# A two-layer trunk on one core: even-odd tiles written in a row, 1/rms by Newton steps, and a resting gate lane

## The chip, the core and the metric

The kernel runs on one core of a Trainium2 chip. The core has a matrix engine (TensorE, PE in the profile), a vector engine (VectorE, DVE), an activation engine (ScalarE, ACT), GpSimd (POOL) and the engine SyncE (SP), whose queue issues the weight DMAs here. Each engine works through its own queue in order and waits on semaphores of the others. SBUF is the memory that all of them share; PSUM holds the sums that TensorE writes. The metric is the device time of one execution in microseconds; lower is better.

## What is computed

272 tokens (16 learned ones in front of 256) of 2048 features go through two layers. The reference, cut to its frame:

```python
def rms_norm(x, g):
    y = x * lax.rsqrt(jnp.mean(x * x, axis=-1, keepdims=True) + EPS)
    return y * g

def mixer_ab(h, ...):                       # layer 0
    q, f, i, g, sx, sb, sc = split_cols(h @ w_in, AB_SIZES)
    o = rms_norm(hgrn2_chunked(q, f, i, lb), out_norm_g) * jax.nn.silu(g)
    yb = sb * causal_depthwise_conv(sc * sx, sconv_w)
    return jnp.concatenate([o, yb], axis=-1) @ w_out

def mixer_cd(h, ...):                       # layer 1
    rx, ry, q, ckv, iq, ik, iw = split_cols(h @ w_in, CD_SIZES)
    u = causal_depthwise_conv(rx, conv_w) + conv_b
    hc = rg_lru(u, w_a, b_a, w_i, b_i, lam) * jax.nn.gelu(ry)
    att = dsa_attention(q, rms_norm(ckv, kv_norm_g), iq, ik, iw, w_uk, w_uv)
    return jnp.concatenate([hc, att], axis=-1) @ w_out

def swiglu(h, w1, w3, w2):
    return (jax.nn.silu(h @ w1) * (h @ w3)) @ w2

for l in range(2):
    h = h + rms_norm(mixer(rms_norm(h, ln_mix_pre[l])), ln_mix_post[l])
    h = h + rms_norm(swiglu(rms_norm(h, ln_ffn_pre[l])), ln_ffn_post[l])
return h[:, 16:]
```

`rg_lru` makes two gates per block of 128 channels, `r = sigmoid(u @ w_a + b_a)` and `ig = sigmoid(u @ w_i + b_i)`, and runs a linear recurrence over time with them. `dsa_attention` selects for each token the best 64 keys by an indexer's scores, and attends to these and to the learned tokens.

## The kernel before

Everything is kept with features on the 128 partitions and tokens along the free dimension: the residual stream is 16 tiles `h[k]` of 128x272. The weights are float32. To keep precision, each weight tile (`raw`, 128x1024, that is four blocks of 128 input rows by 256 output columns) is split into a high and a low part: ScalarE casts it to the rounded format (`whi`, L128), VectorE subtracts (`wlo`, L129). Inputs are split the same way (`xh`, `xl`). Each product is then three matmuls, `whi·xh`, `whi·xl`, `wlo·xh` (L200 to L202 in `group`), so a weight tile is 24 matmuls. There are six buffers for each weight part, seven for `raw`, and eight PSUM banks.

*Even-odd layout.* A split input holds the tokens with even numbers in its first half and those with odd numbers in its second. `woven(t)` is the view that goes through such a tile in the order of tokens (one element of the first half, one of the second, and so on), and `pairs(t)` is a plain tile in the matching shape. TensorE reads the tile through `woven`. In the kernel before the engines also write it through `woven`: the source is read in a row, and consecutive results go alternately to the two halves. The places are `pre` (L305 on ScalarE, L306 on VectorE: the entering input of a stage, 16 tiles per stage), `split_ahead` (L399, L400), `split` with `weave` (L236, L237: hidden tiles of SwiGLU in layer 0, the mixers' outputs), the copies of the values `v` (L1203, L1205), and one sum at the end (L1342).

*Stages.* There are four: mixer and SwiGLU of each layer. `start_stage` brings the residual up to date and splits it, tile by tile, while the first group's matmuls run (`pre`; per tile on VectorE `upd` L439, `h` L440 and `xl` L306, on ScalarE `xh` L305), and then takes the squares for the norm (`squares`). The norm's factor is applied behind the matmuls, so TensorE needs it late: the second group of products carries four hooks, of which the third sums the squares by a matmul (`stat`, L262), forms 1/rms (`inverse_rms`), and the fourth spreads it over partitions by a matmul (`spread`, L288) and copies it (`scale`, L347). `inverse_rms` writes mean square plus epsilon on VectorE (`ms`, L275) and raises it to the power -1/2 on GpSimd (`rms`, L279). It is called for the four stages' own norms, for the norm of the latent in layer 1 (`latent_scale`), and three times with `more` given, for the norm of a stage's output.

*Order.* TensorE runs in the order in which the program is written. On the other engines a scheduler orders the instructions, with `issue_after` as a tool of the program: an instruction made under it is put behind a named one on its engine. `later(i)` makes such a list from `self.urgent` for the weight splits of a group; for groups that start no stage `i` is -1.

*Lanes.* Layer 1's small work is written as generators in three lanes. `pump(n)` takes `n` steps from the first lane that is not empty, between chunks of weights. Lane 0 is the indexer's selection (`select`: `sc`, top-8 rounds L1029, L1030, `bias` L1035), lane 1 the recurrence's gates (`rg_gates`: convolution `u` L965, L967, matmuls `rgr` L971 and `rgi` L972, sigmoids, `rd` L981) and its scan. A lane's "wait" step counts as nothing. The selection is pumped through the groups of the key weights (`wuk`, 1 step per chunk) and the value products (`vacc`, L1199 to L1201).

*End.* The last output halves are summed, normed and written by `finish(b)`, whose DMAs are at L1362. Before the last `finish`, `forms` (L1301) runs 50 matmuls into a PSUM tile that nothing reads.

Of the kernel before, what the change touches and what calls it, by code (L numbers as in the profile page):

```python
# [52 lines left out]

class Trunk:
# [3 lines left out]
    def __init__(self, ctx, tc):  # L58
# [15 lines left out]
        self.copies = []  # L74

# [152 lines left out]
    def split(self, src, n, name, weave=False):  # L228
        hi = self.slot(name + "h", F32R)
        lo = self.slot(name + "l", F32R)  # L230
        if weave:
            hi, lo, src = woven(hi[:, :n]), woven(lo[:, :n]), pairs(src)
            at = slice(None)
        else:
            at = (slice(None), slice(0, n))
        self.nc.scalar.copy(hi[at], src)  # L236
        self.nc.vector.tensor_tensor(lo[at], src, hi[at].bitcast(F32), op=ALU.subtract)  # L237
# [3 lines left out]
    def rsqrt(self, v, shape, mk):  # L241
# [8 lines left out]
        for _ in range(3):  # L250
# [3 lines left out]
            V.scalar_tensor_tensor(b, a, 1.5, y, op0=ALU.add, op1=ALU.mult)  # L254
# [15 lines left out]
    def inverse_rms(self, sums, n, nfeat, more=None):  # L270
# [21 lines left out]
    def streamed(self, j, k, lo_t):  # L292

        return (woven(x[j][:, k, :])[:, lo_t // 2 :, :] for x in (self.xhi, self.xlo))

    def pre(self, k, lo_t, layer, which, update, xs):
# [10 lines left out]
        self.made = a, v  # L307
# [12 lines left out]
        xs.append((xh, xl))  # L320
# [34 lines left out]
    def start_stage(self, m, parts1, parts2, lo_t, layer, which, n, factors, update=None, between=None):  # L355
# [11 lines left out]

        accs1 = self.group(parts1, xg, n, before=before, between=between, begun=begun)
# [23 lines left out]
    def split_ahead(self, m, layer, which, lo_t):  # L392

        nc = self.nc
        for k in range(4):
            g = self.gain(which, layer, k)
            for j, src in (2, self.h[k][:, lo_t:T]), (3, m["m"][k][:, : T - lo_t]):
                xh, xl = self.streamed(j, k, lo_t)
                nc.scalar.activation(xh, pairs(src), AF.Copy, scale=g)  # L399
                nc.vector.scalar_tensor_tensor(xl, pairs(src), g, xh.bitcast(F32), op0=ALU.mult, op1=ALU.subtract)  # L400
# [680 lines left out]
    def mixer_cd(self, a, m):  # L1081
# [96 lines left out]
        for g in range(QFIRST):  # L1178
            queries(g)
        for g in range(4):  # L1180
# [10 lines left out]
        for g in range(2):  # L1191
            raw = self.fetch([(0, 0, wuv[:, 512 * g : 512 * (g + 1)].rearrange("(k p) c -> p k c", p=P))], 2, 512)
            hi, lo = self.whole(raw, 2, 512)
            for i, (t0, n) in enumerate(TOK[T]):
# [8 lines left out]
                S.copy(woven(vs[i][32:48, c] if i == 2 else vs[i][:, c]), pairs(ps[:n, :]))  # L1203
                if i == 1:
                    S.copy(woven(vs[2][:NM, c]), pairs(ps[:NM, :]))  # L1205
                self.pump(1)
        while self.lanes[0]:
            self.pump(1)
        for g in range(QFIRST):
# [205 lines left out]
```

## Time and profile before

| | us |
|---|---|
| device time, median of 3 runs (2305.86 to 2308.21) | 2305.95 |
| the profiled execution | 2310.25 |
| its span | 2308.5 |
| TensorE busy | 2277.6 (99%) |
| VectorE busy | 1511.5 (65%) |
| ScalarE busy | 1127.6 (49%) |
| GpSimd busy | 109.7 (5%) |
| weight DMAs | 414 MB, 179 GB/s read over the span |

The profiled execution took 4.3 us more than the median. TensorE is the engine that works nearly all the time, and the weight stream has room: DMA engines are busy 59% of the span. What a change can win is TensorE's idle time, its time at the lower of its two clock levels, and nothing else unless matmuls are removed. A mean over the span says little here, because the idle time lies in a few places.

### The profile page before, as it was taken

To read this page: it belongs to the slowest core of one execution; us is meant where nothing else is said; L and a number is where in the kernel's file an instruction comes from. 1 tells how busy PE (TensorE), PEld (TensorE's weight loads), DVE (VectorE), ACT (ScalarE), POOL (GpSimd) and SP (SyncE) were. 2 spreads that over 40 slices of the span, in tenths; PEclk is the share of its full clock that TensorE was granted. 3 is DMA by queue.
4 is the path that set the end of the run, shared out by engine and by line. 5 is a ranking of instruction groups with operands and counts; after the bars stand their busy time and mean duration, and the time that the engine had idled before them with its cause. 6 is when DMAs were issued, how large, how long until landed. Compare 5 with 4: busy or idle time off the path is not lost.

```text
span 2308.5 us, 45101 instructions
## 1 busy us (share of the span) xinstructions
PE 2277.6 (99%) x18613; PEld 2217.1 (96%) x18613; DVE 1511.5 (65%) x2441; ACT 1127.6 (49%) x1628; POOL 109.7 (5%) x142
## 2 busy tenths in 40 slices
PE   9999999999999999999999998999999999999999
PEld 8999999989999999999998997999999899989998
DVE  8767677586654555566668798767665456656655
ACT  6443445564444444344456567656444444444443
POOL 1422100000000000000000000200000000000000
PEclk9999999999999999999999999999999999999999
DMA  8554556636666665666564644464666666666663
GB/s 265 155 152 138 156 173 187 200 121 194 188 191 191 189 188 179 194 199 188 176 202 120 207 137 147 146 200 136 205 199 197 204 196 199 199 202 196 198 205 106
DMA packets 402856, 416.98 MB, mean 181 GB/s; under 512 B 15551, under 2 KB 379562, under 8 KB 402650
## 3 DMA queue, kind: packets, MB, share of 16 engines
q1 hardware_dynamic: 402506, 413.95, 59.0%
q8 instruction: 146, 2.39, 0.4%
q14 instruction: 60, 0.49, 0.1%
q10 hardware_dynamic: 144, 0.15, 0.0%
HBM read 411.95 MB, written 2.10 MB: 179 GB/s over the span
## 4 chain that ended last, share of the span: by engine, by line
PE 94%; DVE 3%; ACT 1%; POOL 1%; issue 1%; DMA 0%; SPq 0%; DVEq 0%
PE acc L200 27%; PE acc L201 26%; PE acc L202 26%; PE acc L1261 3%; PE acc L1260 3%; PE acc L1259 3%; DVE xl L306 1%; ACT xh L305 1%; PE lev L702 1%; POOL rms L279 1%; DVE h L440 0%; DVE wlo L129 0%; PE idx L1011 0%; PE forms L1301 0%; PE acc L416 0%
## 5 line engine op out<-in xcount | busy, mean ns | idle before, releaser
L129 DVE TENSOR_TENSOR wlo<-raw,whi 128x1024 fp32r<-128x1024 f32 (+2 forms) x791 | 954.8, 1210 | 655.2 <-ACT whi L128 638.3
L128 ACT CAST whi<-raw 128x1024 fp32r<-128x1024 f32 (+2 forms) x791 | 815.1, 1032 | 1023.3 <-PE acc L201 769.7
L200 PE MATMUL acc<-xh,whi 128*128 128x272 f32 (+1 forms) x4248 | 1193.5, 281 | 3.7 <-DVE pt L556 1.8
L201 PE MATMUL acc<-xl,whi 128*128 128x272 f32 (+1 forms) x4248 | 1184.6, 279 | 7.2 <-DVE xl L306 7.1
L202 PE MATMUL acc<-xh,wlo 128*128 128x272 f32 (+1 forms) x4248 | 1182.2, 278 | 0.0
L201 PEld LDWEIGHTS acc<-xl,whi 128*128 128x128 f32 x4248 | 811.2, 191 | 11.9 <-DVE xl L306 11.3
L200 PEld LDWEIGHTS acc<-xh,whi 128*128 128x128 f32 x4248 | 811.2, 191 | 9.5 <-ACT xh L305 3.9
L202 PEld LDWEIGHTS acc<-xh,wlo 128*128 128x128 f32 x4248 | 811.3, 191 | 0.0
L200 PE MATMUL acc<-hidh,whi 128*128 128x272 f32 x704 | 196.7, 279 | 0.0
L201 PE MATMUL acc<-hidl,whi 128*128 128x272 f32 x704 | 196.6, 279 | 0.0
L202 PE MATMUL acc<-hidh,wlo 128*128 128x272 f32 x704 | 196.6, 279 | 0.0
L1259 PE MATMUL acc<-whi,hidh 128*128 128x512 f32 (+1 forms) x380 | 139.0, 366 | 0.0
L1261 PE MATMUL acc<-wlo,hidh 128*128 128x512 f32 (+1 forms) x380 | 138.3, 364 | 0.0
L1260 PE MATMUL acc<-whi,hidl 128*128 128x512 f32 (+1 forms) x380 | 138.3, 364 | 0.0
L200 PEld LDWEIGHTS acc<-hidh,whi 128*128 128x128 f32 x704 | 133.2, 189 | 0.0
L201 PEld LDWEIGHTS acc<-hidl,whi 128*128 128x128 f32 x704 | 133.2, 189 | 0.0
L202 PEld LDWEIGHTS acc<-hidh,wlo 128*128 128x128 f32 x704 | 133.2, 189 | 0.0
L1261 PEld LDWEIGHTS acc<-wlo,hidh 128*128 128x128 f32 x380 | 72.1, 190 | 8.6
L1259 PEld LDWEIGHTS acc<-whi,hidh 128*128 128x128 f32 x380 | 72.1, 190 | 8.4
L1260 PEld LDWEIGHTS acc<-whi,hidl 128*128 128x128 f32 x380 | 72.1, 190 | 8.3
L279 POOL TENSOR_TENSOR rms<-ms,minus_half 128x3 f32<-128x3 f32 (+1 forms) x8 | 18.1, 2268 | 1080.4 <-DVE ms L277 929.2
L305 ACT ACTIVATE xh<-h,pt 128x272 fp32r<-128x272 f32 (+1 forms) x48 | 33.5, 760 | 22.2 <-DVE h L440 21.7
(366 smaller groups left out, 2180.2 us busy)
## 6 DMA issues: line engine op xcount, KB each, us to landing
raw<-in_ffn_w_dram SPq DMA_DIRECT2D x518, 512.0 KB, 3.7
raw<-in_ab_w_in_dram SPq DMA_DIRECT2D x110, 512.0 KB, 3.6
raw<-in_cd_w_in_dram SPq DMA_DIRECT2D x68, 512.0 KB, 4.3
raw<-in_ab_w_out_dram SPq DMA_DIRECT2D x28, 512.0 KB, 3.5
raw<-in_cd_w_out_dram SPq DMA_DIRECT2D x28, 512.0 KB, 4.0
raw<-in_ffn_w_dram SPq DMA_DIRECT2D x17, 256.0 KB
raw<-in_ab_w_out_dram SPq DMA_DIRECT2D x8, 256.0 KB, 3.0
raw<-in_cd_w_out_dram SPq DMA_DIRECT2D x8, 256.0 KB, 4.5
```

The lines of the kernel that those rows point to most:

```text
L128: nc.scalar.copy(hi[at], raw[at])
L129: nc.vector.tensor_tensor(lo[at], raw[at], hi[at].bitcast(F32), op=ALU.subtract)
L200: nc.tensor.matmul(o, lhsT=hi[:, kk, c : c + m], rhs=xh, start=k == 0, stop=False)
L201: nc.tensor.matmul(o, lhsT=hi[:, kk, c : c + m], rhs=xl, start=False, stop=False)
L202: nc.tensor.matmul(o, lhsT=lo[:, kk, c : c + m], rhs=xh, start=False, stop=k == nk - 1)
L279: i = self.nc.gpsimd.tensor_tensor(r[:, :w], self.ms[:, :w], self.minus_half[:, :w], op=ALU.pow)
L305: a = nc.scalar.activation(xh, pairs(h), AF.Copy, scale=g)
L306: v = nc.vector.scalar_tensor_tensor(xl, pairs(h), g, xh.bitcast(F32), op0=ALU.mult, op1=ALU.subtract)
L702: nc.tensor.matmul(ps[:M, j * half : (j + 1) * half], lhsT=k[:, j * P : j * P + M], rhs=upper(qh[:, j * P : (j + 1) * P]), start=True, sto ...
L1259: self.nc.tensor.matmul(o, lhsT=xh, rhs=wh, start=k == 0, stop=False)
L1260: self.nc.tensor.matmul(o, lhsT=xl, rhs=wh, start=False, stop=False)
L1261: self.nc.tensor.matmul(o, lhsT=xh, rhs=wl, start=False, stop=k == nk - 1)
```

## The change

Four things are edited.

1. *Layout written in a row.* `halves(t)` is a tile as two contiguous halves, and `apart(t)` a plain tile with its even elements first. The splits now write through `halves` and read the source through `apart`, with a stride of two elements. What is stored where is the same, and TensorE reads it through `woven` as before. `pre` and `split_ahead` share a new helper `enter`.
2. *1/rms by Newton steps.* Without `more`, `inverse_rms` calls `rsqrt` (a function that the kernel has for another norm): a shift and a subtraction on the bits give a first guess, three Newton steps follow, eleven small VectorE instructions, each on the result of the one before. Its last instruction is kept in `self.hold`, and until the next stage starts `later(-1)` puts the weight splits of ordinary groups behind it (their VectorE instruction `wlo`; the cast on ScalarE has nothing to be put behind there).
3. *The gate lane rests.* During the groups of the key weights and the value products `self.awake` is 1, so `pump` serves lane 0 alone; then 3 again.
4. *`forms` is gone*, with its 50 matmuls.

```diff
+def apart(t):
+    return t.rearrange("p (j a) -> p a j", a=2)
+def halves(t):
+    return t.rearrange("p (a j) -> p a j", a=2)
...
     def pump(self, n):
-        for lane in self.lanes:
+        for lane in self.lanes[: self.awake]:
...
                 if i >= first:
                     ctx.enter_context(self.tc.issue_after(ins.ins))
+            if self.hold and i < 0:
+                ctx.enter_context(self.tc.issue_after(self.hold.ins))
             yield
...
         if weave:
-            hi, lo, src = woven(hi[:, :n]), woven(lo[:, :n]), pairs(src)
-            at = slice(None)
+            h, l, src = halves(hi[:, :n]), halves(lo[:, :n]), apart(src)
+            hi, lo = woven(hi[:, :n]), woven(lo[:, :n])
...
-        r, w = self.tiny("rms"), len(TOK[n])
+        w = len(TOK[n])
+        if more is None:
+            r = self.rsqrt(self.ms[:, :w], (P, w), lambda name, dtype: self.tiny(name, (P, 8), dtype))
+            self.hold = self.last_root
+            return r
+        r = self.tiny("rms")
         i = self.nc.gpsimd.tensor_tensor(r[:, :w], self.ms[:, :w], self.minus_half[:, :w], op=ALU.pow)
-        if more is not None:
-            self.urgent.append((6, i))
+        self.urgent.append((6, i))
...
+    def enter(self, j, k, lo_t, src, g):
+        h, l = (halves(x[j][:, k, :])[:, :, lo_t // 2 :] for x in (self.xhi, self.xlo))
+        a = self.nc.scalar.activation(h, apart(src), AF.Copy, scale=g)
+        v = self.nc.vector.scalar_tensor_tensor(l, apart(src), g, h.bitcast(F32), op0=ALU.mult, op1=ALU.subtract)
+        return a, v
...
-        xh, xl = self.streamed(k // 4, k % 4, lo_t)
-        a = nc.scalar.activation(xh, pairs(h), AF.Copy, scale=g)
-        v = nc.vector.scalar_tensor_tensor(xl, pairs(h), g, xh.bitcast(F32), op0=ALU.mult, op1=ALU.subtract)
+        a, v = self.made = self.enter(k // 4, k % 4, lo_t, h, g)
...
+        self.hold = None
         accs1 = self.group(parts1, xg, n, before=before, between=between, begun=begun)
...
+        self.awake = 1
         for g in range(4):
             for t in self.group([self.pair(wuk, 256 * g)], cx, T, 1):
...
-                S.copy(woven(vs[i][32:48, c] if i == 2 else vs[i][:, c]), pairs(ps[:n, :]))
+                S.copy(halves(vs[i][32:48, c] if i == 2 else vs[i][:, c]), apart(ps[:n, :]))
...
         while self.lanes[0]:
             self.pump(1)
+        self.awake = 3
...
-                V.tensor_tensor(woven(t), pairs(src), woven(t), op=ALU.add)
+                V.tensor_tensor(halves(t), apart(src), halves(t), op=ALU.add)
...
-            if b:
-                self.forms(hid)
             finish(b)
```

The edits move instructions on their engines, and the line numbers of the changed kernel run some 11 to 21 lines higher. On VectorE, at the norm of layer 0's SwiGLU, this stood in a row before (`wlo` are low parts of the next weight tiles, `ms` the mean square, `z` the first use of the norm's factor; the numbers only tell the tiles of one kernel apart):

```order
L129 TENSOR_TENSOR wlo_6714<-raw_6711,whi_6713 128x1024
L129 TENSOR_TENSOR wlo_6744<-raw_6741,whi_6743 128x1024
L129 TENSOR_TENSOR wlo_6774<-raw_6771,whi_6773 128x1024
L275 TENSOR_SCALAR ms_99<-stat_6635 128x2
L275 TENSOR_SCALAR ms_99<-stat_6635 16x1
L129 TENSOR_TENSOR wlo_6804<-raw_6801,whi_6803 128x1024
L129 TENSOR_TENSOR wlo_6850<-raw_6847,whi_6849 128x1024
L129 TENSOR_TENSOR wlo_6880<-raw_6877,whi_6879 128x1024
L902 TENSOR_TENSOR z_6675<-far_6484,scale_6673 128x272
```

In the changed kernel there stands, behind the two `ms`:

```order
L260 TENSOR_SCALAR rs_sh_6658<-ms_99 128x3
L261 TENSOR_SCALAR rs_g_6659<-rs_sh_6658 128x3
L265 TENSOR_TENSOR rs_a_6662<-rs_g_6659 128x3
L266 SCALAR_TENSOR_TENSOR rs_a_6662<-rs_a_6662,ms_99 128x3
L267 SCALAR_TENSOR_TENSOR rs_y_6663<-rs_a_6662,rs_g_6659 128x3
L265 TENSOR_TENSOR rs_a_6667<-rs_y_6663 128x3
L266 SCALAR_TENSOR_TENSOR rs_a_6667<-rs_a_6667,ms_99 128x3
L267 SCALAR_TENSOR_TENSOR rs_y_6668<-rs_a_6667,rs_y_6663 128x3
L265 TENSOR_TENSOR rs_a_6672<-rs_y_6668 128x3
L266 SCALAR_TENSOR_TENSOR rs_a_6672<-rs_a_6672,ms_99 128x3
L267 SCALAR_TENSOR_TENSOR rs_y_6673<-rs_a_6672,rs_y_6668 128x3
L140 TENSOR_TENSOR wlo_6748<-raw_6745,whi_6747 128x1024
L140 TENSOR_TENSOR wlo_6778<-raw_6775,whi_6777 128x1024
```

Three low parts that stood ahead of `ms` have gone behind the last Newton step, and the eleven small instructions stand where GpSimd's work was; the low part that comes first there, of the chunk whose matmuls follow `spread`, stood before among those ahead of `ms`.

On TensorE, the last pair of gate matmuls stood before inside the value products (`vacc`):

```order
L1201 MATMUL vacc_17350<-whi_17338,cl_16229 128x512
L971 MATMUL rgr_17359<-u_17317,rgw_15852 128x272
L972 MATMUL rgi_17360<-u_17317,rgw_15852 128x272
L1199 MATMUL vacc_17372<-whi_17338,ch_16223 16x512
L1200 MATMUL vacc_17372<-wlo_17339,ch_16223 16x512
```

In the changed kernel it stands between two tiles of transposed attention weights (`pT`), behind the first round of `qk`:

```order
L1085 MATMUL pT_17622<-ident_90,s_17490 128x128
L1086 MATMUL pT_17622<-ident_90,s_17483 16x16
L1087 MATMUL pT_17622<-ident_90,s_17490 48x16
L991 MATMUL rgr_17632<-u_17557,rgw_15903 128x272
L992 MATMUL rgi_17633<-u_17557,rgw_15903 128x272
L1083 MATMUL pT_17645<-ident_90,s_17513 128x128
```

The pair before it (`rgr_17280` in the kernel before) has gone the same way, from the products of the key weights to a place between two `qk` tiles, and no gate matmul is left in the key and value products.

## Rows read from the trace of the kernel before

**Rows 1.** The page, part 1: busy us, share of the span, instructions.
```profile
PE 2277.6 (99%) x18613; PEld 2217.1 (96%) x18613; DVE 1511.5 (65%) x2441; ACT 1127.6 (49%) x1628; POOL 109.7 (5%) x142
```

**Rows 2.** Waits of TensorE over the whole span: releaser, us in total, times, longest us.
```profile
PE spread L288 <- POOL rms L279: 9.5, 3, 3.6
PE acc L201 <- DVE xl L306: 7.1, 20, 0.9
PE rgr L971 <- issue: 6.0, 1, 6.0
PE acc L200 <- DVE pt L556: 1.8, 1, 1.8
PE acc L200 <- ACT xh L305: 1.5, 6, 0.4
```

**Rows 3.** Stretches: busy time and instructions by engine, granted clock, DMA share, GB/s.
```profile
521.50:527.40 5.90, 5.83 (x25) 5.47 (x26) 2.99 (x8) 1.47 (x4) 0.92 (x2) 0.50 0.90 293
...
1272.00:1278.30 6.30, 6.28 (x28) 5.92 (x29) 2.49 (x7) 0.54 (x2) 0.00 (x0) 0.50 0.93 293
...
1398.90:1404.60 5.70, 5.70 (x13) 3.30 (x14) 1.23 (x3) 3.98 (x7) 0.00 (x0) 0.50 0.52 156
...
1625.10:1630.00 4.90, 4.90 (x30) 4.90 (x30) 2.85 (x8) 1.92 (x5) 0.00 (x0) 0.65 1.08 358
```

**Rows 4.** Timeline of layer 0's first SwiGLU norm: start us, us, engine, line.
```profile
513.79 3.49 DVE L129 TENSOR_TENSOR wlo<-raw,whi 128x1024 fp32r<-128x1024 f32 x3
514.36 0.63 PE L262 MATMUL stat<-ones,preacc 128*128 128x1 f32 x6
517.20 0.20 DVE L275 TENSOR_SCALAR ms<-stat 128x2 f32<-128x2 f32 x2
517.33 3.47 DVE L129 TENSOR_TENSOR wlo<-raw,whi 128x1024 fp32r<-128x1024 f32 x3
517.48 4.04 POOL L279 TENSOR_TENSOR rms<-ms,minus_half 128x3 f32<-128x3 f32 x1 [40.02 <-DVE ms L275]
521.57 0.90 PE L288 MATMUL spread<-ident,rms 128*128 128x128 f32 x3 [3.61 <-POOL rms L279]
```

**Rows 5.** Lines by form: busy us, mean ns of one, idle before.
```profile
L275 DVE TENSOR_SCALAR ms<-stat 128x2 f32<-128x2 f32 x5 | 0.8, 162 | 1.2 <-PE stat L262 1.2
L305 ACT ACTIVATE xh<-h,pt 128x272 fp32r<-128x272 f32 x32 | 22.6, 770 | 15.3 <-DVE h L440 15.1
L306 DVE SCALAR_TENSOR_TENSOR xl<-h,pt,xh 128x272 fp32r<-128x272 f32 x32 | 21.0, 707 | 2.5 <-ACT xh L305 1.4
L967 DVE SCALAR_TENSOR_TENSOR u<-rx,pt,u 128x269 f32<-128x269 f32 x8 | 4.0, 494 | 0.1
L454 ACT ACTIVATE m<-acc,pt 128x272 f32<-128x272 f32 x16 | 7.8, 489 | 0.0
L728 DVE TENSOR_TENSOR F<-f 128x136 f32<-128x136 f32 x8 | 2.3, 289 | 0.0
L440 DVE TENSOR_TENSOR h<-h,upd 128x272 f32<-128x272 f32 x32 | 13.1, 435 | 0.1
L1316 ACT COPY part<-acc 128x256 f32<-128x256 f32 x16 | 5.2, 382 | 4.4 <-PE acc L1261 4.4
```

**Rows 6.** Timeline of the last gate pair inside the value products.
```profile
1393.50 1.85 DVE L981 RECIPROCAL rd<-rd 128x272 f32<-128x272 f32 x1
...
1397.13 1.22 DVE L129 TENSOR_TENSOR wlo<-raw,whi 128x1024 fp32r<-128x1024 f32 x1
1398.26 0.50 DVE L967 SCALAR_TENSOR_TENSOR u<-rx,pt,u 128x269 f32<-128x269 f32 x1
1398.86 1.24 PE L971 MATMUL rgr<-u,rgw 128*128 128x272 f32 x2 [6.00 <-issue]
```

**Rows 7.** Timeline of the end.
```profile
2296.61 8.35 SPq L1362 DMA_DIRECT2D out_dram<-wide  x10
...
2298.57 6.88 PE L1301 MATMUL forms<-whi,hidh 128*128 128x272 f32 x50
```

More of the change, by code (lines that the diff above doesn't have):

```diff
@@ L231, in split @@
         if weave:
-            hi, lo, src = woven(hi[:, :n]), woven(lo[:, :n]), pairs(src)
-            at = slice(None)
-        else:
-            at = (slice(None), slice(0, n))
-        self.nc.scalar.copy(hi[at], src)
-        self.nc.vector.tensor_tensor(lo[at], src, hi[at].bitcast(F32), op=ALU.subtract)
+            h, l, src = halves(hi[:, :n]), halves(lo[:, :n]), apart(src)
+            hi, lo = woven(hi[:, :n]), woven(lo[:, :n])
+        else:
+            h, l = hi[:, :n], lo[:, :n]
+        self.nc.scalar.copy(h, src)
+        self.nc.vector.tensor_tensor(l, src, h.bitcast(F32), op=ALU.subtract)
         return hi, lo
@@ L253, in rsqrt @@
             V.scalar_tensor_tensor(a, a, -0.5, v, op0=ALU.mult, op1=ALU.mult)
-            V.scalar_tensor_tensor(b, a, 1.5, y, op0=ALU.add, op1=ALU.mult)
+            self.last_root = V.scalar_tensor_tensor(b, a, 1.5, y, op0=ALU.add, op1=ALU.mult)
             y = b
@@ L292, in streamed @@
     def streamed(self, j, k, lo_t):
-        return (woven(x[j][:, k, :])[:, lo_t // 2 :, :] for x in (self.xhi, self.xlo))
+        return [woven(x[j][:, k, :])[:, lo_t // 2 :, :] for x in (self.xhi, self.xlo)]
+    def enter(self, j, k, lo_t, src, g):
[3 more added lines that the diff above has]
+        return a, v
     def pre(self, k, lo_t, layer, which, update, xs):
@@ L319, in pre @@
                 self.copies = []
-        xs.append((xh, xl))
+        xs.append(self.streamed(k // 4, k % 4, lo_t))
     def squares(self, lo_t):
@@ L366, in before @@
             xg.append(tuple(x[:, (nn - n) // 2 :, :] for x in xs[k]))
+        self.hold = None
         accs1 = self.group(parts1, xg, n, before=before, between=between, begun=begun)
@@ L397, in split_ahead @@
             for j, src in (2, self.h[k][:, lo_t:T]), (3, m["m"][k][:, : T - lo_t]):
-                xh, xl = self.streamed(j, k, lo_t)
-                nc.scalar.activation(xh, pairs(src), AF.Copy, scale=g)
-                nc.vector.scalar_tensor_tensor(xl, pairs(src), g, xh.bitcast(F32), op0=ALU.mult, op1=ALU.subtract)
+                self.enter(j, k, lo_t, src, g)
     def ahead(self, m, parts, n, nn):
@@ L1202, in mixer_cd @@
                 c = slice(512 * g, 512 * (g + 1))
-                S.copy(woven(vs[i][32:48, c] if i == 2 else vs[i][:, c]), pairs(ps[:n, :]))
+                S.copy(halves(vs[i][32:48, c] if i == 2 else vs[i][:, c]), apart(ps[:n, :]))
                 if i == 1:
-                    S.copy(woven(vs[2][:NM, c]), pairs(ps[:NM, :]))
+                    S.copy(halves(vs[2][:NM, c]), apart(ps[:NM, :]))
                 self.pump(1)
@@ L1208, in mixer_cd @@
             self.pump(1)
+        self.awake = 3
         for g in range(QFIRST):
@@ L1252, in by_tokens @@
                 hi, lo = parts[ci]
-                self.flat = hi.rearrange("p k c -> p (k c)")
                 for kk in range(kc):
@@ L1275, in turn @@
         yield
-    def forms(self, hid):
-        f = self.flat
-        x = hid[0][0][:, :P]
-        ps = self.misc("forms")
-        far = lambda d, n: f[:, : 2 * d].rearrange("p (a j) -> p j a", a=2)[:, : n // 2, :]
-        for rhs, n in (
-            (f[:, 0:272], 272),
-            (far(128, 256), 256),
-            (far(136, 272), 272),
-            (far(256, 512), 512),
-            (far(240, 272), 272),
-            (far(160, 256), 256),
-            (far(130, 256), 256),
-            (f[:, 0:256].rearrange("p (a j) -> p j a", a=4), 256),
-            (f[:, 0:256].rearrange("p (a j c) -> p j a c", a=2, c=2), 256),
-            (f[:, 0:256].rearrange("p (a j c) -> p j a c", a=2, c=8), 256),
-        ):
-            o = ps[:, :n]
-            if len(rhs.shape) == 3:
-                o = o.rearrange("p (j a) -> p j a", a=rhs.shape[2])
-            elif len(rhs.shape) == 4:
-                o = o.rearrange("p (j a c) -> p j a c", a=2, c=rhs.shape[3])
-            for _ in range(5):
-                self.nc.tensor.matmul(o, lhsT=x, rhs=rhs, start=True, stop=True)
     def output_part(self, a, layer, row0, hid, part, pi, out):
```

1 line of the change is left out of this document (removed).

## The prediction, made before the changed kernel ran

> **What bounds the kernel now.** I read the busy times first: TensorE works 99% of the span, every other engine two thirds or less [rows 1]. So only two things can be won without taking away products: the moments in which TensorE stands still, and the stretches in which its clock is at the lower level. The list of TensorE's waits gives the first. GpSimd's power holds up `spread` three times for 9.5 us, the gate matmul `rgr` stands 6.0 us once, and the inputs that enter a stage, `xl` and `xh`, hold up products 26 times for 8.6 us; `pt`, the turned table of gains, costs 1.8 us once [rows 2]. The stretches give the second. Behind four of these stalls, and nowhere else in the span, the granted clock is 0.50 or has a mean of 0.65, that is 1.2 GHz of 2.4 for all or part of the stretch [rows 3]. What a stretch costs is its length times (1 - clock): 5.9 x 0.50 = 2.95, 6.3 x 0.50 = 3.15, 5.7 x 0.50 = 2.85 and 4.9 x 0.35 = 1.7 us. The third of these follows `rgr`, the other three the three norms. So the norms cost 9.5 + 7.8 = 17.3 us and the gate 6.0 + 2.85 = 8.85 us.
>
> Why are the norms late? At layer 0's SwiGLU the sum `stat` is begun at 514.36, but `ms` comes at 517.20, because three low parts stand in front of it on VectorE; then GpSimd's power runs 4.04 us, beside three more low parts, and ends shortly after the last of them; TensorE has waited 3.61 us [rows 4]. Both delays come from the low parts. The wait that ends last is GpSimd's; without it TensorE would have gone on at 521.57 - 3.61 = 517.96.
>
> **Part 1, the norms.** In the new order nothing stands between the last sum of squares and `ms`. So `ms` starts when `stat` is done, some 0.75 us behind its start: 515.1 (514.36 plus its 0.63 and a hand-over). The eleven Newton instructions work on 128x3. The nearest row is `ms` itself, 162 ns for 128x2 [rows 5]; with some 30 ns between dependent ones I take 0.19 us each, 2.1 us in all, and 0.25 for the two `ms`. 1/rms is ready at 515.1 + 0.25 + 2.1 = 517.45, half a microsecond before TensorE comes for it. The bounds: eleven at 0.16 with nothing between are 1.8 us; at the 435 ns of an instruction with 272 elements (`h` [rows 5]) they are 4.8 us, `spread` would come at 520.2, and 2.2 of the 3.61 us stay.
>
> What is late next: the low part of the chunk behind `spread`, which is now queued behind the Newton steps. It starts at 517.45 and takes 1.16 to 1.22 us ([rows 4, 6]), so it is there at 518.7. TensorE has `spread` done half a microsecond behind 517.96 (0.90 us at the half clock, [rows 4]) and can issue the first `whi` products; the low part is wanted near 518.4. That is a new wait of 0.3 us here, and by the same count some 0.35 and 0.45 at the other two norms: 1.1 us in all. The low parts that follow have a chunk of 24 matmuls each to run beside, and VectorE has time for them. A stall of a third of a microsecond stands among the many of its size in the start phases, which have no stretch at the lower clock behind them. So I take both the wait and the clock as won: 17.3 - 1.1 = **16.2 us**, between 4 us (Newton at the upper bound, so part of the waits stays and the clock falls as before) and 17.3.
>
> The first stage's norm is not waited for now. There the Newton steps push low parts back for a cost of 0.5 to 0.9 us, but fewer low parts stand ahead of the instruction that makes `pt`, and most of its 1.8 us of wait [rows 2] should go: **+0.7 us**, between -1 and +1.5. At the latent's norm one low part goes behind the Newton steps, and no wait is shown now: **-0.5 us**, between -1.2 (a whole low part) and 0. The casts on ScalarE are not held, so the buffers of raw weights come free by VectorE alone: a delay of some 2 us per norm with the weight stream at under 60% of its engines, which I cost at nothing.
>
> **Part 2, the gate lane.** `rgr` stands still until the last `u`, made at 1398.26 on VectorE, behind a reciprocal of 1.85 us and two low parts [rows 6]; these in turn come behind the bias that the selection makes. The value products leave TensorE nothing else to do. With the lane at rest the pair goes between `pT` tiles, where the attention part has products on either side. I followed the order of VectorE and ScalarE through that part with the durations of the rows: the last `u` is ready over 1 us before TensorE comes to `rgr`, and the second round's softmax keeps some slack. ScalarE has to change its function table and take eight square roots there, which is the thinnest place. I take the whole **8.85 us**, between 0 (the stall only moves) and 8.85.
>
> **Part 3, the layout.** Writing alternately is dear: `xh` takes 770 ns and `xl` 707 for 272 elements, while the same operations with a scale vector and results in a row take 489 (`m`) and 494 (`u`) [rows 5]. What is not seen is the new read with stride two. On VectorE there is a row: 128x136 with both inputs at stride two takes 289 ns, and going by `h` (435 for 272) and the fixed part of some 150 ns a plain one would take about the same. On ScalarE only a read from PSUM at stride two is seen, 382 ns for 256 elements, no dearer than plain ones; none from SBUF. So `xh` lies between 0.49 us and, if strided reads are as dear as alternating writes, 0.77, and I take 0.49; `xl` likewise 0.50.
>
> The Trainium skill (SBUF — State Buffer, on "cachelines") says that SBUF goes at full rate as long as two accesses in a row fall in one line of 16 bytes. Two float32 values at stride two do, and two written to the two halves do not; by that rule ScalarE's read from SBUF is as free as I take it. The same page says that PSUM's lines are 8 bytes and that a pattern with gaps slows a matmul there; carried over to reads it would make the first stage's inputs no faster, some 1 us less than my sum. The row of 382 ns does not show such a cost, and the measurement decides.
>
> In 48 steps (three stages with 16 tiles; the first stage's come from PSUM) VectorE saves 48 x 0.21 = 10 us. TensorE can gain from this only where it waits, 8.6 us [rows 2], and VectorE's loop also carries four low parts per stage, which stay. I take 2 us per stage, **6 us**, between 0 and 10. The rest of the layout's saving (SwiGLU's hidden tiles, `v`, outputs) lies beside TensorE's work and gives 0.
>
> **Part 4, `forms`.** Its 50 matmuls end at 2298.57 + 6.88 = 2305.45. But the last output DMAs are issued from 2296.61 on until 2304.96 [rows 7], behind `finish`, which doesn't wait for `forms`, and their landing ends the span at 2308.5. TensorE is free of its last product at 2298.6. So the removal gives **0**, at most the half microsecond between the two ends.
>
> **Sum.** 16.2 + 0.7 - 0.5 + 8.85 + 6 + 0 = 31.3 us off the profiled execution's 2310.25, that is 2279. That execution stands 4.3 us over the median; taken from the median 2305.95 it is **2275 us**.
>
> **Rivals.**
> A. *The norm's wait only changes its name.* The Newton steps are slow, or the low parts behind them come so late that TensorE stalls there for over a microsecond and the clock still falls. For it: all low parts of the next groups are behind one chain; against it: the row of 162 ns. Part 1 gives 4 instead of 16.2: 2287 us. Chance 0.13.
> B. *Strided reads cost what alternating writes cost.* Part 3 gives 0: 2281 us. For it: ScalarE shows no such read from SBUF; against: VectorE's 289 ns. Chance 0.14.
> C. *The gate's stall moves into the attention part.* For it: the table change, and three kinds of work on ScalarE in a row; against: TensorE has other products there. Part 2 gives 0: 2284 us. Chance 0.08.
> D. *Slower.* Reads at stride two are far dearer than alternating writes, so that the 48 steps of the start phases set the pace of the stage. The place is `xh` and `xl`, on ScalarE and VectorE; it turns the sign when a step grows by over 25/48 = 0.5 us, that is from about 1.25 us apiece, since parts 1 and 2 give 25 us. At 1.8 us each it costs 48 x 1.05 = 50 us: 2306 + 50 - 25 = 2331 us. No row is near this. Chance 0.06.
> E. *The edits don't decide.* A and C together, and the layout gives little: within 0.2% of before, about 2302 us. Chance 0.04.
>
> **How the numbers follow.** The forecast has 0.55, with its own range 2267 to 2282 (part 3 at either bound, part 1 a little less). A to C lie at 2281 to 2287, and two of them together at 2290 to 2293. A range from 2264 to 2291 leaves out D, E and the tails, about 2 in 10. A measurement of this kernel can tell some 0.2% (4.6 us) from no change. Faster by more than that: forecast, A, B and C, 0.90, less 0.01 for two of them at once. Within: 0.04. Slower: D and mishaps that I don't see, 0.07.
>
> **What would show it.** Right: no wait of `spread` on `rms`, and the three stretches at the lower clock gone; eleven instructions near 0.16 us behind `ms`; waits of a few tenths on the low part behind `spread`; no wait at `rgr`; `xh` and `xl` near 0.5 us. `forms` gone and the time from TensorE's last product to the span's end as it was, about 10 us. Wrong: a clock of 0.5 behind any norm, `xh` still at 0.7 us or more, a wait of microseconds on `pT` or `rgr` in the attention part, or start phases that are no shorter though `xl` is.

## The result and the profile after

The changed kernel takes 2278.53 us, median of four runs (2277.14 to 2279.76), against 2307.08 us of the kernel before, timed beside it (2305.86 to 2310.12): a ratio of 0.9875, interval 0.986 to 0.9889. That is 28.5 us off, with 2275 us forecast and a range of 2264 to 2291. The profiled execution took 2278.28 us with a span of 2276.6. The sum was nearly right; two of its terms were not, in opposite directions.

The page's busy times of the changed kernel, in the form of [rows 1]:

```profile
PE 2258.6 (99%) x18563; PEld 2203.0 (97%) x18563; DVE 1491.2 (66%) x2496; ACT 1097.1 (48%) x1628; POOL 95.9 (4%) x137
```

TensorE's waits in it, to be laid beside [rows 2]. Its lines run 11 to 21 higher: `spread` is now L305, the three products are L213 to L215, the low part is L140.

```profile
PE acc L215 <- DVE wlo L140: 3.0, 2, 2.6
PE acc L214 <- DVE xl L317: 1.7, 5, 0.7
...
PE spread L305 <- DVE rs_y L267: 0.7, 1, 0.7
PE acc L213 <- DVE pt L576: 0.3, 1, 0.3
```

The 9.5 us at three norms, the 6.0 us at `rgr` and most of the start phases' 8.6 us are gone. One wait of 2.6 us is new, on a low part. The 0.7 us at `spread` is the first stage's norm.

At layer 0's SwiGLU norm the timeline now reads thus (some of the eleven small rows between are left out); it answers [rows 4].

```profile
510.24 0.63 PE L275 MATMUL stat<-ones,preacc 128*128 128x1 f32 x6
...
510.98 0.21 DVE L288 TENSOR_SCALAR ms<-stat 128x2 f32<-128x2 f32 x2 [1.13 <-PE stat L275]
511.23 0.17 DVE L260 TENSOR_SCALAR rs_sh<-ms 128x3 int32<-128x3 int32 x1
511.43 0.17 DVE L261 TENSOR_SCALAR rs_g<-rs_sh 128x3 int32<-128x3 int32 x1
...
513.21 0.16 DVE L267 SCALAR_TENSOR_TENSOR rs_y<-rs_a,rs_y 128x3 f32<-128x3 f32 x1
513.28 3.50 DVE L140 TENSOR_TENSOR wlo<-raw,whi 128x1024 fp32r<-128x1024 f32 x3
513.69 0.54 PE L305 MATMUL spread<-ident,rs_y 128*128 128x128 f32 x3
```

`ms` comes 0.74 us behind `stat`'s start (0.75 forecast), the eleven steps take 513.37 - 511.23 = 2.14 us (2.1 forecast), and `spread` finds 1/rms ready, at the full clock.

The new wait lies in layer 1's mixer, behind that stage's norm. Timeline of the changed kernel, and the stretches around the wait (busy us and instructions of PE, PEld, DVE, ACT, POOL, then the granted clock, DMA share, GB/s):

```profile
1257.94 1.41 DVE L1110 TENSOR_TENSOR iqs<-acc,scale 128x256 f32<-128x256 f32 x4
...
1259.26 1.21 DVE L140 TENSOR_TENSOR wlo<-raw,whi 128x1024 fp32r<-128x1024 f32 x1
...
1260.50 5.38 DVE L1123 TENSOR_TENSOR iq<-iqs,iq 64x256 fp32r<-64x256 f32 x12
...
1265.91 3.83 DVE L140 TENSOR_TENSOR wlo<-raw,whi 128x1024 fp32r<-128x1024 f32 x4
```

```profile
1267.19 0.38 PE L215 MATMUL acc<-xh,wlo 128*128 128x256 f32 x1 [2.62 <-DVE wlo L140]
```

```profile
1268.30:1271.70 3.40, 3.40 (x19) 3.40 (x18) 2.27 (x5) 0.57 (x1) 0.00 (x0) 0.50 0.95 297
```

Twelve splits of the indexer's queries stand in a row on VectorE for 5.4 us, in front of the low part that TensorE wants next. TensorE waits 2.62 us, and the clock is at its lower level (1.2 GHz) for 3.4 us behind it, which costs half of that. Before the end this is the only such stretch in the changed kernel.

The split of the entering inputs, lines by form in the changed kernel (busy us, mean ns of one | idle before), against L305 and L306 of [rows 5]:

```profile
L316 ACT ACTIVATE xh<-h,pt 128x272 fp32r<-128x272 f32 x40 | 21.1, 554 | 13.2 <-DVE h L460 12.4
L317 DVE SCALAR_TENSOR_TENSOR xl<-h,pt,xh 128x272 fp32r<-128x272 f32 x40 | 19.1, 499 | 0.4 <-ACT xh L316 0.4
L316 ACT ACTIVATE xh<-xT,pt 128x272 fp32r<-128x272 f32 x16 | 6.6, 481 | 0.8 <-PE xT L668 0.8
```

VectorE's went from 707 to 499 ns, ScalarE's from 770 to 554, a little above the 490 forecast; from PSUM (`xT`) it is 481. (The 40 are the 32 of [rows 5] and eight of `split_ahead`, which now share the line.)

Busy time in the three start phases that the table below begins with, before and after (sums of the three stretches):

```profile
sum 108.40, PE 100.34 PEld 94.40 DVE 103.08 ACT 76.47 POOL 0.00; mean PE 33.45 PEld 31.47 DVE 34.36 ACT 25.49 POOL 0.00
sum 97.84, PE 95.79 PEld 93.13 DVE 94.24 ACT 69.25 POOL 0.95; mean PE 31.93 PEld 31.04 DVE 31.41 ACT 23.08 POOL 0.32
```

VectorE works 95% of these phases before and 96% after, ScalarE 71%.

To see where the two profiled executions differ I compared the same stretches. Their spans differ by 31.9 us:

| stretch, between the same matmuls | before | after | difference |
|---|---|---|---|
| three start phases, `spread` of the stage's input to `stat` | 108.4 | 97.8 | -10.6 |
| `stat` to `spread`, three norms | 19.9 | 9.9 | -10.0 |
| behind the norm in layer 0's SwiGLU, to the next `spread` | 708.1 | 705.5 | -2.6 |
| behind the norm in layer 1's mixer, to the latent's `spread` | 41.4 | 43.7 | +2.2 |
| the latent's `spread` to the next stage (holds `rgr`) | 269.6 | 260.6 | -9.0 |
| behind the norm in layer 1's SwiGLU, to the last product | 673.4 | 672.4 | -1.0 |
| first stage: start to `stat`, to `spread`, to the next stage | 477.7 | 477.45 | -0.2 |
| last product to the end of the span | 10.05 | 9.35 | -0.7 |

### The profile page after: what moved, and what is told of

Read it like the earlier page. It is cut to its first block, busy times and chain, and to the rows that moved or that the text cites. A ratio compares the mean times of both kernels' runs of the same rounds, so it can differ in the third digit from the quotient of the medians.

```text
span 2276.6 us, 45023 instructions
## 1 busy us (share of the span) xinstructions
PE 2258.6 (99%) x18563; PEld 2203.0 (97%) x18563; DVE 1491.2 (66%) x2496; ACT 1097.1 (48%) x1628; POOL 95.9 (4%) x137
## 4 chain that ended last, share of the span: by engine, by line
PE 64%; issue 31%; DVE 3%; DMA 1%; ACT 0%; SPq 0%; POOL 0%; ACTq 0%; DVEq 0%; POOLq 0%
PE acc L213 20%; PE acc L215 20%; PE acc L214 20%; PE lev L722 1%; DVE wlo L140 1%; DVE xl L317 1%; DMA raw<-in_ab_w_in_dram 0%; DVE upd L459 0%; DVE h L460 0%; PE idx L1031 0%; DVE wide L1356 0%; PE qk L1067 0%; DMA mrow<-in_meta_tokens_dram 0%; PE stat L275 0%; PE acc L436 0%
## 5 line engine op out<-in xcount | busy, mean ns | idle before, releaser
L140 DVE TENSOR_TENSOR wlo<-raw,whi 128x1024 fp32r<-128x1024 f32 (+2 forms) x791 | 953.1, 1208 | 644.1 <-ACT whi L139 628.5
L213 PE MATMUL acc<-xh,whi 128*128 128x272 f32 (+1 forms) x4248 | 1190.1, 280 | 0.6 <-DVE pt L576 0.3
L215 PE MATMUL acc<-xh,wlo 128*128 128x272 f32 (+1 forms) x4248 | 1180.2, 278 | 3.2 <-DVE wlo L140 3.0
L213 PEld LDWEIGHTS acc<-xh,whi 128*128 128x128 f32 x4248 | 808.7, 190 | 5.1 <-issue 0.9
L215 PEld LDWEIGHTS acc<-xh,wlo 128*128 128x128 f32 x4248 | 808.8, 190 | 4.1 <-DVE wlo L140 4.0
L213 PE MATMUL acc<-hidh,whi 128*128 128x272 f32 x704 | 196.7, 279 | 0.0
L215 PE MATMUL acc<-hidh,wlo 128*128 128x272 f32 x704 | 196.5, 279 | 0.0
L213 PEld LDWEIGHTS acc<-hidh,whi 128*128 128x128 f32 x704 | 133.2, 189 | 0.0
L215 PEld LDWEIGHTS acc<-hidh,wlo 128*128 128x128 f32 x704 | 133.2, 189 | 0.0
L297 POOL TENSOR_TENSOR rms<-ms,minus_half 128x3 f32<-128x3 f32 (+1 forms) x3 | 2.4, 811 | 959.4 <-DVE ms L290 959.4
```

The source lines that it names most:

```text
L140: nc.vector.tensor_tensor(lo[at], raw[at], hi[at].bitcast(F32), op=ALU.subtract)
L213: nc.tensor.matmul(o, lhsT=hi[:, kk, c : c + m], rhs=xh, start=k == 0, stop=False)
L215: nc.tensor.matmul(o, lhsT=lo[:, kk, c : c + m], rhs=xh, start=False, stop=k == nk - 1)
```

## The experiments

The first theory was that the parts add up as in this table. Each run is compared with runs of the kernel before made beside it, whose medians are 2306.3 to 2307.9.

**The layout alone.** The changed kernel, with these lines taken out again:

```diff
-        if more is None:
-            r = self.rsqrt(...); self.hold = self.last_root; return r
...
-        self.awake = 1
```

> The kernel before with the layout written in a row (and without the 50 unread matmuls); 1/rms stays on GpSimd, nothing is held, the gate lane stays awake. Theory: the start phases (spread to stat, three stages) shrink by 10.6 us together as in the trace of the changed kernel, because what sets them is VectorE's and ScalarE's work per tile, and nothing else of this part shows on TensorE: about 2296 us, three waits of spread on rms and four stretches at the lower clock as before. Rival: the gain of the start phases leans on the norms' new order (fewer low parts there), then under 6 us: 2301 us or more.

Measured: 2294.2 us against 2306.3, ratio 0.9944 (0.9929 to 0.9959), 12.1 us off. Its waits:

```profile
PE spread L302 <- POOL rms L293: 10.2, 4, 3.7
PE rgr L988 <- issue: 6.0, 1, 6.0
PE acc L214 <- DVE xl L314: 1.6, 4, 0.7
```

The norms and the gate wait as before, the inputs hardly. The three start phases take 97.9 us in its trace (32.80, 32.78 and 32.28), as in the changed kernel, though the norms are the old ones. So the layout is worth 10 to 12 us by itself, twice the 6 forecast, and the rival falls.

**The Newton steps and the low parts behind them, alone.** Layout and lane as before:

```diff
-        h, l = (halves(x[j][:, k, :])[:, :, lo_t // 2 :] for x in (self.xhi, self.xlo))
-        a = self.nc.scalar.activation(h, apart(src), AF.Copy, scale=g)
+        h, l = self.streamed(j, k, lo_t)
+        a = self.nc.scalar.activation(h, pairs(src), AF.Copy, scale=g)
...
-        self.awake = 1
```

> The kernel before with Newton steps and the low parts behind them (and without the 50 unread matmuls); layout alternating, gate lane awake. Theory: the three waits of spread go, and a new one comes in layer 1's mixer, where a low part stands behind twelve splits of the indexer's queries on VectorE: 10 to 12 us, about 2296 us, with the stall of about 2.6 us and one stretch at the lower clock there. Rival (as predicted, 16 us): no stall there without the faster start phase, 2291 us. Rival: the norm's waits only change place, under 5 us, 2302 us.

Measured: 2299.16 us against 2306.3, ratio 0.9964 (0.9951 to 0.9977): 7.1 us off, less than the 10 to 12 expected. The stall in the mixer is there, and the waits on `spread` are gone but for the first stage's:

```profile
PE acc L215 <- DVE wlo L140: 3.0, 2, 2.6
PE spread L305 <- DVE rs_y L267: 1.3, 1, 1.3
```

So the stall in the mixer doesn't come from the quicker start phase. It belongs to this part. By the rows, 9.5 us of waits on `spread`, some 3 to 4 us of lower clock (from the further profiles below) and 1.5 us at `pt` are won, and 3.0 + 1.7 us at low parts and 1.3 us at the first `spread` lost, which makes 8 to 9 us; the measured 7.1 has an interval of 5.3 to 11.3.

**The gate lane alone.** The kernel before with `self.awake` and nothing else:

```diff
-        for lane in self.lanes:
+        for lane in self.lanes[: self.awake]:
...
+        self.awake = 1
         for g in range(4):
             for t in self.group([self.pair(wuk, 256 * g)], cx, T, 1):
```

> The kernel before with the gate lane at rest during key weights and value products, nothing else. Theory: the stall of 6.0 us at rgr and the stretch at the lower clock behind it go, nothing new comes in the attention part: 9.0 us, about 2298 us. Rival: with alternating writes ScalarE is busier, and the attention part waits a few us: 2301 us or more.

Measured: 2297.98 us against 2306.3, ratio 0.9962 (0.9949 to 0.9975): 8.3 us off. No wait on `rgr` is left in its list, and none in the attention part came in its place. The three parts alone give 12.1 + 7.1 + 8.3 = 27.5 us, together they gave 28.5: within their intervals, some 3 us each way, they add up.

**The query splits spread out.** In the changed kernel the twelve splits become a generator that is run between weight chunks:

```diff
-        index_queries(accs1 + accs2)
-        index_queries(self.group([self.pair(w, CIQ + 768)], xr, NL))
+        first = index_queries(accs1 + accs2)
+        some = lambda n, it: [next(it, None) for _ in range(n)]
+        some(1, first)
+        accs = self.group([self.pair(w, CIQ + 768)], xr, NL, hooks={i: lambda: some(2, first) for i in range(3)})
+        second = index_queries(accs)
+        some(1, second)
```

> The changed kernel, with the twelve splits of the indexer's first queries on ScalarE and VectorE made one by one between the next weight chunks instead of in a row. Theory: the stall of 2.6 us behind layer 1's first norm comes from these twelve (5.4 us) in front of a low part in VectorE's queue; with five in front of it the stall and the stretch at the lower clock behind it go: 4.3 us off, about 2274 us. Rival: the low parts are late because the norm holds them all back, then the wait stays above 2 us: 2278 us.

Measured: 2275.15 us (2274.5 to 2275.45). This run mixed up the order of the indexer's heads; a second version, with each query kept at its head's place, is the same work:

> The changed kernel with the indexer's query splits made between weight chunks as in the run before on this, each query now kept at its own head's place, so that all is computed as in the reference. Theory: same order of work, same time, 2275 us, no stretch at the lower clock before the end. Rival: none; a time over 2277 us would mean that the earlier run's gain was not the stall's.

Measured: 2274.72 us (2274.18 to 2275.82) against 2307.63, ratio 0.9856 (0.9839 to 0.9872). In its timeline five splits stand in a row instead of twelve, the wait on a low part in the mixer is gone (0.4 us is the one in layer 1's SwiGLU), and no stretch at the lower clock is left before the end.

```profile
1261.01 2.22 DVE L1123 TENSOR_TENSOR iq<-iqs,iq 64x256 fp32r<-64x256 f32 x5
```

```profile
PE acc L215 <- DVE wlo L140: 0.4, 1, 0.4
```

The stall cost 3.8 us (4.3 expected), and what TensorE waited for is the low part behind the twelve splits in VectorE's queue. The part of the clock in this cost differs between executions: in the run with the other tiles alternating (below) the same wait of 2.62 us has no stretch at the lower clock behind it.

```profile
1268.58 0.38 PE L215 MATMUL acc<-xh,wlo 128*128 128x256 f32 x1 [2.62 <-DVE wlo L140]
```

```profile
1268.50:1271.90 3.40, 3.32 (x29) 3.32 (x30) 3.40 (x7) 0.63 (x1) 0.00 (x0) 1.00 0.60 176
```

**The power kept, with the low parts behind `ms`.** What of the norm's cost is GpSimd's, what the queue's?

```diff
-                self.nc.vector.tensor_scalar(v, sums[at], 1.0 / nfeat, EPS, op0=ALU.mult, op1=ALU.add)
+                self.hold = self.nc.vector.tensor_scalar(v, sums[at], 1.0 / nfeat, EPS, op0=ALU.mult, op1=ALU.add)
...
-        if more is None:
-            r = self.rsqrt(...); self.hold = self.last_root; return r
```

> The changed kernel with 1/rms on GpSimd's power again, but the low parts of the following groups held back to behind ms, so that the power starts as early as the Newton steps do. Theory: the power is slow because low parts run on VectorE beside it; it will take 3 us or more again, end with the low parts, and spread will wait 1 to 3 us at three stages, with a lower clock behind some of them: 4 to 10 us over the changed kernel, 2283 to 2289 us. Rival: only the place in VectorE's queue counted, the power takes 0.9 us when it starts early, spread doesn't wait: 2278 us.

Measured: 2272.86 us (2272.05 to 2275.78) against 2307.51, ratio 0.9852 (0.9837 to 0.9867): the fastest of all, 5.7 us below the changed kernel's median. My theory fell. Timeline at the same norm:

```profile
510.59 0.63 PE L275 MATMUL stat<-ones,preacc 128*128 128x1 f32 x6
...
511.48 4.63 DVE L140 TENSOR_TENSOR wlo<-raw,whi 128x1024 fp32r<-128x1024 f32 x4
511.63 1.78 POOL L293 TENSOR_TENSOR rms<-ms,minus_half 128x3 f32<-128x3 f32 x1 [34.06 <-DVE ms L288]
...
514.04 0.54 PE L302 MATMUL spread<-ident,rms 128*128 128x128 f32 x3
```

Four low parts run beside the power, and it takes 1.78 us, not 4.04. It is ready 0.6 us before `spread`, and the first low part is ready before that. No wait on `rms` or on a low part is in the list of this kernel. In the mixer VectorE's rows show why no low part is late there, with the twelve splits still in a row:

```profile
1252.98 3.50 DVE L140 TENSOR_TENSOR wlo<-raw,whi 128x1024 fp32r<-128x1024 f32 x3
...
1258.45 1.22 DVE L140 TENSOR_TENSOR wlo<-raw,whi 128x1024 fp32r<-128x1024 f32 x1
1259.70 5.37 DVE L1120 TENSOR_TENSOR iq<-iqs,iq 64x256 fp32r<-64x256 f32 x12
```

All four low parts of that group of products are ahead of the splits; behind the Newton steps three are. From `spread` of this norm to the latent's it takes 38.5 us here and 43.7 in the changed kernel, which is 5.2 of the 5.7 us. The rival named 0.9 us for the power, which isn't right either: where no low part runs beside it (the stage outputs' norms) its rows say 0.70 to 0.86.

**The Newton steps without holding the low parts.**

```diff
             r = self.rsqrt(...)
-            self.hold = self.last_root
             return r
```

> The changed kernel without putting the low parts behind the Newton steps; the scheduler then mixes six low parts in front of and between the eleven small instructions. Theory: 1/rms comes some 5 us later, spread waits 3 to 5 us at three stages, the stall in layer 1's mixer behind the norm goes: 6 to 12 us over the changed kernel, 2285 to 2291 us. Rival: Newton's steps alone are the gain, under 2 us over it: 2280 us.

Measured: 2296.97 us (2295.92 to 2298.36) against 2307.51, ratio 0.9955 (0.994 to 0.997); 18.4 us over the changed kernel, more than the 6 to 12 expected: `spread` waits at four stages, the first included (4.4 us), and four stretches at the lower clock, 17.1 us together, lie behind these waits. Its waits, and one of the places where a low part stands in the chain:

```profile
PE spread L304 <- DVE rs_y L267: 17.8, 4, 4.9
```

```profile
519.43 0.15 DVE L260 TENSOR_SCALAR rs_sh<-ms 128x3 int32<-128x3 int32 x1
519.50 1.21 DVE L140 TENSOR_TENSOR wlo<-raw,whi 128x1024 fp32r<-128x1024 f32 x1
520.64 0.15 DVE L261 TENSOR_SCALAR rs_g<-rs_sh 128x3 int32<-128x3 int32 x1
```

At layer 0's norm six low parts stand in front of and in the chain. Where one gets between two of the eleven steps, the next step starts 1.21 us later instead of 0.20. By the waits on `spread` (17.8 us against 9.5 in [rows 2]) the Newton steps without the order edge are worse than the power was.

**The order of the low parts alone.** The kernel before with the edit of the run with the power kept, and nothing else (the 50 unread matmuls are out too):

> The kernel before (without the 50 unread matmuls), with one edit: behind a stage's own norm the low parts of the following groups are held back to behind ms; the power stays on GpSimd, the layout alternating, the gate lane awake. Theory, formed on the run with the power kept: the place of the low parts in VectorE's queue is the whole of the norms' cost, the power is ready before TensorE comes, and no low part is late behind it: 10 us of waits and some 3 us of lower clock go, 2294 us, with rows of 1.6 to 1.8 us for the power. Rival: with alternating writes the power is held up by the low parts again as before (4 us rows), spread still waits, 2299 us or more, no better than Newton's steps alone.

Measured: 2293.09 us (2292.76 to 2293.38) against 2307.87, ratio 0.9933 (0.9916 to 0.9951): 14.8 us off (interval 11.3 to 19.4), about twice what the Newton steps with the low parts behind them gave; the two kernels lie 6.1 us apart, and their ranges don't touch. No wait on `rms` or on a low part is in its list. The power is short here too:

```profile
516.60 1.78 POOL L293 TENSOR_TENSOR rms<-ms,minus_half 128x3 f32<-128x3 f32 x1 [37.99 <-DVE ms L288]
...
1607.98 1.65 POOL L293 TENSOR_TENSOR rms<-ms,minus_half 128x2 f32<-128x2 f32 x1 [36.71 <-DVE ms L288]
```

**The other tiles alternating again.** `split`, the copies of `v` and the last sum write through `woven` as before; only `enter` stays:

```diff
-            h, l, src = halves(hi[:, :n]), halves(lo[:, :n]), apart(src)
-            hi, lo = woven(hi[:, :n]), woven(lo[:, :n])
+            hi, lo, src = woven(hi[:, :n]), woven(lo[:, :n]), pairs(src)
+            h, l = hi, lo
```

> The changed kernel, with alternating writes again in the hidden tiles, the mixers' outputs, the copies of v and the one sum at the end; only the inputs that enter a stage stay in a row. Theory: these lie beside TensorE's work, ScalarE and VectorE get some 20 us busier each and the time stays: 2278 to 2280 us. Rival: part of the layout's 10.6 us comes from them, then 2281 us or more.

Measured: 2278.37 us (2277.16 to 2278.98). No change: all of the layout's gain is in the inputs that enter a stage.

**The 50 matmuls back.** `forms` and its call as in the kernel before.

> The changed kernel with the 50 unread matmuls at the end put back. Theory: the output's last DMAs end behind them, no change: 2278 to 2279 us. Rival: the 0.7 us by which the stretch from the last product to the end became shorter comes from them: 2279.3 us. Rival: the whole 6.7 us: 2285 us.

Measured: 2279.16 us (2277.67 to 2280.41), 0.6 us over the changed kernel with ranges that overlap. So no cost of theirs is shown, and the 6.7 us are excluded; the first rival's 0.7 us are too little to be told from none.

**The kernel before, profiled twice more.**

> The kernel before, unchanged, one more profiled execution. Theory: the stalls at spread and rgr come again at the same length, but the stretches at the lower clock behind them don't: 0, 3.4 or 6.8 us each, so that the clock's part of the cost differs by some us from one execution to the next. Rival: each stall brings the same stretch as in the first profile (6.8, 6.8, 6.8, 3.4 us).

> The same once more: theory and rival as for the second profile of the kernel before.

Both have the same stalls (`spread` 9.5 us in 3, `rgr` 6.0). They took 2306.69 and 2306.08 us, against 2310.25 of the execution that the prediction was read from. Stretches of the second and the third profile, chosen where either has the lower clock behind the norms:

```profile
520.10:526.80 6.70, 5.17 (x22) 4.80 (x23) 3.75 (x9) 1.47 (x4) 2.38 (x2) 0.50 1.02 328
...
1272.40:1275.70 3.30, 3.30 (x30) 3.30 (x31) 2.48 (x7) 0.91 (x2) 0.00 (x0) 1.00 1.09 357
...
1622.60:1625.90 3.30, 3.30 (x18) 3.30 (x17) 2.85 (x8) 0.80 (x3) 0.00 (x0) 0.50 1.11 366
```

```profile
521.50:524.80 3.30, 3.30 (x14) 2.93 (x15) 1.50 (x4) 1.47 (x4) 0.84 (x1) 0.50 1.03 353
...
1272.40:1275.70 3.30, 3.30 (x18) 3.30 (x17) 1.88 (x6) 0.09 (x1) 0.00 (x0) 0.50 1.02 328
...
1622.60:1625.90 3.30, 3.30 (x31) 3.30 (x31) 2.15 (x7) 1.78 (x5) 0.00 (x0) 1.00 1.07 357
```

The windows lie just inside the stretches. The second has 6.8 us at the lower clock behind layer 0's norm, none behind the mixer's and 3.4 behind the last; the third has 3.4, 3.4 and none. Half of the time in which TensorE works there is lost (in the second's first stretch it works 5.17 us, the rest is still the wait): 7.8 us in the first profile, 4.2 in the second, 3.3 in the third. Behind `rgr` all three have 6.8 us. So the same stall brings stretches of different length, or none, and in these three profiles that is about the 4 us by which their times differ.

## Why the prediction was right, and where it was not

*The norms* were the largest term, 16.2 us, and the most mis-sized: alone they gave 7.1. The Newton steps came as worked out, and all three waits on `spread` went. Two steps failed. The first: "The low parts that follow have a chunk of 24 matmuls each to run beside, and VectorE has time for them." At two norms that held (waits of 0.4 us and less on the first low part). In the mixer, six `iqs` and twelve `iq` instructions stand among these low parts, and I had read only the one low part behind the chain; 1.1 us of new waits were in the sum, 3.0 us of waits and 1.7 us of lower clock came. With the chain one of them went there: in the run with the power kept, four low parts come between `ms` and the twelve splits; here, with 2.1 us of VectorE gone to the Newton steps, three do, and the fourth is the one that TensorE waits for. The second step: "So I take both the wait and the clock as won", with the clock's 7.8 us read from one execution and taken off the median of others. That execution was the one with the longest such stretches of three; 3.3 to 4.2 us was there to win in the others. "That execution stands 4.3 us over the median" was in the text, and I did not ask what the 4.3 us were.

*The reason for the late norm* was read only half. I put both delays down to low parts, in front of `ms` and beside the power, and took it that the power had to go. The place in the queue alone gives 14.8 us with the power kept (and the unread matmuls gone), about what the prediction gave to the whole part. The Newton steps bring a chain of 2.1 us on VectorE, behind which every low part waits; the power takes 1.7 us on an engine that is idle. A bound that I did not work out was the power with a free start.

*The gate lane* came out as predicted: 8.85 forecast, 8.3 measured alone, 9.0 in the stretch. No wait moved into the attention part.

*The layout* was forecast with 6 us between 0 and 10, and gave 10.6 in the stretches and 12.1 alone (where the unread matmuls are gone too). The reads at stride two cost VectorE what was taken (499 ns, 500 taken); on ScalarE they are 0.06 us dearer (554 ns, 490 taken). The step that failed is "TensorE can gain from this only where it waits, 8.6 us". The list of waits dropped by 6.9 us, and the start phases by 10.6: the list counts too little. TensorE's busy time in these phases fell too, by 4.6 us (100.3 to 95.8) for the same products: a matmul behind a wait has a row of 0.38 us instead of 0.28, and the next one starts 0.22 us behind it instead of 0.11. VectorE's saving of 48 x 0.21 = 10 us was the better measure, since VectorE's loop set the pace of those phases: it is busy 95% of them, and in the run with the order of low parts alone a start phase with 3.4 us at TensorE's lower clock in it took 36.27 us, against 36.21 in the kernel before without such a stretch. The saving in all other tiles gave 0, as predicted.

*The first stage, the latent and `forms`* were priced at +0.7, -0.5 and 0: the first stage gave 0.2 (its wait on `pt` went from 1.8 to 0.3, and `spread` waits 0.7), the latent's stretch from `stat` to `spread` is 0.4 us longer (7.55 against 7.14), near the price, though no wait is in the list, and for `forms` no cost is shown.

With the norms 9 us too high, the layout 6 too low and the rest within 1, the sum was 31.3 against 28.5 measured. Its nearness is in part luck: the two errors cancel. Against the profiled execution, from which its terms were read, 31.3 stands beside 31.9 in the table, with the same two errors there (the norms' four rows give 11.4, the start phases 10.6). Of the rivals, A and C together come to 2296 us by their own prices, not to 2290 to 2293; nothing hangs on it. What the place of a low part in VectorE's queue costs is shown by experiment; why the power needs 4 to 5 us in the kernel before and 1.7 us beside as many low parts in the others is not. In the kernel before, at the three norms, three or four low parts follow `ms` and the power ends 0.6 to 0.7 us behind the last; at the latent's norm, where one low part follows, it takes 1.78 us and ends 0.7 us behind that one. In the others it ends some 0.7 us behind the first of four. The rows show no pause between the low parts in either order: they start 1.13 to 1.14 us apart in the kernel before and in the others. In the others the second low part waits on two or three more semaphores, which may leave a moment free; that was not tried by itself.

## What to carry to other kernels

Before an operation on the critical path is replaced, give it a free start: look at what stands in front of it in its producer's queue, and move that first. When a wait goes, read the next ten microseconds of every queue that feeds the engine, every instruction by name, as far as the engine gets in that time; work that was hidden under the old wait is the next wait. Take the cost of a lower clock from several executions, not from the one that happens to be profiled.

## What the runs showed of the hardware

- The lower clock behind one and the same stall differs between executions: behind layer 0's norm (3.6 us of waiting) 6.8, 6.8 and 3.4 us in three profiles of one kernel, behind the mixer's 6.8, 0 and 3.4. A wait of 2.62 us had 3.4 us behind it in the changed kernel and none in the run with the other tiles alternating.
- A long single stall isn't needed. In the run with the order of low parts alone the clock is at 0.50 from 1234.0 to 1237.4, in a start phase whose single waits just before were 0.19 to 0.35 us:

```profile
1228.00:1234.00 6.00, 4.74 (x33) 3.79 (x32) 5.55 (x13) 4.76 (x7) 0.00 (x0) 1.00 0.00 0
1234.10:1237.40 3.30, 3.30 (x17) 3.30 (x17) 3.00 (x9) 2.09 (x3) 0.00 (x0) 0.50 0.02 5
```

  So "the many of its size in the start phases, which have no stretch at the lower clock behind them" was true of the profile that I read, and not in general.
- A read at stride two costs ScalarE about 40 ns on 272 elements from SBUF (554 against 512 for an operation with a scale vector read and written in a row, `y` from `u`), VectorE next to nothing (499 against 494), and nothing shows from PSUM (481 against 489 of `m`). Writing alternately to two halves instead of reading at stride two costs 216 ns more on ScalarE (770 against 554) and 208 on VectorE (707 against 499). The Trainium skill (SBUF — State Buffer, on "cachelines") says that accesses in a row to one 16-byte line go at full rate; VectorE's rows agree, and ScalarE's do but for the 40 ns. The 8-byte lines of PSUM, which it ties to matmuls, don't show in ScalarE's reads.
- Dependent instructions on 128x3 start 0.20 us apart on VectorE (the first of eleven at 511.23, the last at 513.21).
